# Emitting side work in step with the matrix products, and loading four groups of small vectors earlier

## The chip, the cores and the metric

The kernel runs on one core of one Trainium2 chip. The metric is device time in microseconds (us), the median of several runs of the whole kernel: 2437.35 us before the change, from 2432.09 to 2441.47 over three runs. The profile is of one further execution, which took 2433.36 us.

## The reference

The program is two networks, one after the other, on 256 tokens of width 1024 in float32. The first has two layers and a second stream of 256 context tokens; its even layer mixes with windowed attention beside a gated linear recurrence, its odd layer with retention. The second has two layers that mix gated delta-rule heads with windowed attention, each followed by a feed-forward part with a short convolution. What the change touches is this:

```python
# both networks: every sublayer is scaled, shifted and gated by vectors of a condition
m_lat = jnp.split((cond_lat @ mod_w[layer] + mod_b[layer])[:, None, :], 6, axis=-1)
h_lat = modulate(rms_norm(x, norm_g[layer, 0]), m_lat[0], m_lat[1])   # h * (1 + scale) + shift
x = x + m_lat[2] * y_lat
x = x + m_lat[5] * swiglu(modulate(...), ffn_w_in[layer], ffn_w_out[layer])
# even mixer: the query and key heads (64 wide) are normalised and multiplied by head weights
k_ctx = kv_heads(pc['a_k'], qk_g[1])
q_lat = apply_rope(attn_q_heads(p['a_q'], qk_g[0]), cos, sin)
```

The product of the condition with `mod_w` (called modulation here) has 1024 rows and 6144 columns per layer. The second network has the same with `w_ada`. It also has short vectors per layer: the norm weights of its attention's queries and keys (64 each), 16 sinks, and two vectors of 8 for the decay of its delta-rule heads.

## The kernel before

Every matrix product keeps float32 accuracy by three TensorE passes: each operand is split into a high and a low part, and hi·hi, hi·lo and lo·hi are added in PSUM (`mm3`, L190 to L192; the same three passes by hand in `fm_block`, L272 to L274). A weight tile of 128x1024 (512 KB) is fetched by a DMA that SyncE (SP) issues (`wload`, L177, tile `raw`, four buffers), ScalarE (ACT) casts its high part (`whi`, L181), and VectorE (DVE), or for some tiles GpSimd (POOL), subtracts to get the low part (`wlo`, L183).

The first modulation is a prologue on TensorE (`modulate_first`): four quarters `q`, each with `mbig` tiles of `mod_w`, followed by the tiles of the even layer's input weight for the same quarter of the contraction. A second set, for the even layer's later sublayers, runs by `mod_round` (L365). The modulation of the three layers that follow (called M1, M2, M3 in the code; three rounds of 2048 columns each) is spread over the even layer's feed-forward part, the odd layer and the odd layer's feed-forward part. It is a generator of 288 pieces (`mod_sums`): each fetches a 256 KB tile `mraw` (four buffers) and adds it, scaled by the condition, to an accumulator `macc` of 128x512, on DVE (L387, 280 of them) or, for the first of each eight, on ACT (L389). After 32 pieces a round ends: matmuls with a tile of ones (L393) add up the four accumulators of the round, a bias is added (`mraw`, L414), and the row is transposed into columns (L420, L423). There are four `macc` buffers, so the DVE additions of the next round wait for those matmuls.

`fill()` steps the generator. It is called once per weight tile, at the end of `wload`, and steps by `self.rate` pieces: 2.7 in the even layer's feed-forward part, 1.3 in the odd layer, 0.9 in the feed-forward part after it.

The order of instructions on each engine is not written by hand: the program emits them in a sequence, and a scheduler of the compiler places them per engine, with the emission as its priority. Each engine then runs its list in order. SP's list of DMA issues is such a list too, and the transfers of one queue are served in the order of issue.

The feed-forward part works in groups of hidden columns: gate and up products with the tokens as columns (`fm_block`), then a down-projection in two halves of 512 output columns (`proj_tm`), each into four PSUM banks, one per 128 tokens. DVE multiplies each bank by the gate (`res`, L494), which frees it.

In the even mixer `even_prep` (L850) loads the head weights `qkg` right before they are used: two DMAs that repeat 64 numbers over heads and partitions, 128x8x64 and 128x2x64. POOL multiplies by them (`qn`, L867). In the second network `bcast_rows` (L600) loads each short vector over 128 partitions where its layer begins: `sgq`, `sgk`, `ssink`, `alog` and `dtb`.

## Time and profile before

| | |
|---|---|
| median of three runs | 2437.35 us (2432.09 to 2441.47) |
| the profiled execution | 2433.36 us |
| its span, first to last instruction | 2431.5 us |
| TensorE matmuls busy | 2318.9 us (95%) |
| TensorE weight loads busy | 1954.7 us (80%) |
| VectorE busy | 1501.8 us (62%) |
| ScalarE busy | 1034.9 us (43%) |
| GpSimd busy | 751.5 us (31%) |
| mean granted TensorE clock | 0.978 of full speed |
| DMA | 399.77 MB, mean 164 GB/s |

TensorE is the engine that hardly rests: what it does not do in 2431.5 us is 112.6 us. So what an edit can save lies in these idle stretches, and in those where the granted clock is below 1. Busy time of the other engines counts only where TensorE waits for them. In the rows further on, a timeline row gives the start of an instruction (or of several alike, xN), how long they took, the engine, the line, and in brackets how long the engine was idle before it and what ended that.

### The profile page before, as it was taken

How to read it: one execution, taken by the hardware profiler on the slowest of the kernel's cores; microseconds unless marked ns; L12 is line 12 of the kernel's file. 1: busy time of each engine (PE TensorE's matmuls, PEld its weight loads, DVE VectorE, ACT ScalarE, POOL GpSimd, SP SyncE). 2: the span in 40 equal slices, each digit the busy share in tenths (PEclk: the TensorE clock that was granted, in tenths of full speed). 3: DMA queues.
4: the chain of work that ended last, by engine and by line, in shares of the span. 5: the costliest groups of instructions: out<-in, count | busy, mean ns of one | idle time of the engine just before them, and what ended most of it. 6: DMA issues, size and time to landing. Idle time of an engine off the chain costs nothing.

```text
span 2431.5 us, 38487 instructions
## 1 busy us (share of the span) xinstructions
PE 2318.9 (95%) x15032; PEld 1954.7 (80%) x15032; DVE 1501.8 (62%) x2398; ACT 1034.9 (43%) x1626; POOL 751.5 (31%) x554
## 2 busy tenths in 40 slices
PE   7889999998998999998999999998999999999999
PEld 6667778776786987877988987678997887778997
DVE  3677748767357747456434887356764888445763
ACT  3545425321223433334444654244444654344442
POOL 1544431112113123223443462133122462214112
PEclk9999999999999999999999999999999999999999
DMA  8333336777466737456655543254665552344664
GB/s 277 110 121 106 122 123 216 240 228 235 126 208 217 250 119 234 139 163 212 188 184 148 158 126 116 87 161 148 191 186 147 162 135 82 116 130 154 186 189 139
DMA packets 305898, 399.77 MB, mean 164 GB/s; under 512 B 38052, under 2 KB 203860, under 8 KB 303668
## 3 DMA queue, kind: packets, MB, share of 16 engines
q1 hardware_dynamic: 303540, 397.18, 52.5%
q8 instruction: 118, 1.93, 0.3%
q14 instruction: 64, 0.52, 0.1%
q10 hardware_dynamic: 2176, 0.13, 0.1%
HBM read 394.51 MB, written 2.74 MB: 163 GB/s over the span
## 4 chain that ended last, share of the span: by engine, by line
PE 74%; DVE 9%; DMA 8%; issue 4%; POOL 3%; ACT 1%; SPq 1%; POOLq 0%; DVEq 0%; ACTq 0%
PE acc L190 11%; PE acc L192 11%; PE acc L191 11%; PE acc L272 9%; PE acc L274 9%; PE acc L273 9%; DMA mraw<-in_w_ada_dram 5%; DVE macc L387 2%; DVE wlo L183 2%; DMA qkg<-in_attn_qk_norm_g_dram 1%; PE sm L1763 1%; PE rc L1751 1%; DVE pre L1609 1%; PE sm L1765 1%; PE rc L1753 1%
## 5 line engine op out<-in xcount | busy, mean ns | idle before, releaser
L181 ACT CAST whi<-raw 128x1024 fp32r<-128x1024 f32 (+1 forms) x528 | 550.7, 1046 | 615.1 <-PE acc L192 322.4
L183 DVE TENSOR_TENSOR wlo<-raw,whi 128x1024 fp32r<-128x1024 f32 x379 | 510.8, 1351 | 428.9 <-ACT whi L181 418.3
L183 POOL TENSOR_TENSOR wlo<-raw,whi 128x1024 fp32r<-128x1024 f32 (+1 forms) x149 | 369.3, 2478 | 1042.2 <-ACT whi L181 1023.8
L272 PE MATMUL acc<-hTh,whi 128*128 128x256 f32 (+1 forms) x1888 | 591.7, 313 | 12.6 <-DVE res L494 11.2
L274 PE MATMUL acc<-hTh,wlo 128*128 128x256 f32 (+1 forms) x1888 | 590.9, 313 | 2.8 <-DVE wlo L183 2.8
L273 PE MATMUL acc<-hTl,whi 128*128 128x256 f32 (+1 forms) x1888 | 589.4, 312 | 0.0
L272 PEld LDWEIGHTS acc<-hTh,whi 128*128 128x128 f32 x1888 | 357.9, 190 | 42.8 <-ACT whi L181 14.3
L274 PEld LDWEIGHTS acc<-hTh,wlo 128*128 128x128 f32 x1888 | 357.7, 190 | 29.8 <-DVE wlo L183 3.8
L273 PEld LDWEIGHTS acc<-hTl,whi 128*128 128x128 f32 x1888 | 358.1, 190 | 24.6 <-issue 3.2
L190 PE MATMUL acc<-whi,hTh 128*128 128x512 f32 (+2 forms) x992 | 334.4, 339 | 2.3 <-DVE rt L1126 0.7
L192 PE MATMUL acc<-whi,hTl 128*128 128x256 f32 (+2 forms) x992 | 331.1, 336 | 1.4 <-DVE hTl L168 0.9
L191 PE MATMUL acc<-wlo,hTh 128*128 128x512 f32 (+2 forms) x992 | 332.1, 336 | 0.0
L387 DVE SCALAR_TENSOR_TENSOR macc<-mraw,sil,macc 128x512 f32<-128x512 f32 x280 | 237.1, 857 | 78.6 <-DMA mraw<-in_w_ada_dram 45.2
L190 PEld LDWEIGHTS acc<-whi,hTh 128*128 128x128 f32 x992 | 187.9, 190 | 28.6 <-issue 6.1
L192 PEld LDWEIGHTS acc<-whi,hTl 128*128 128x128 f32 x992 | 187.0, 189 | 24.7 <-issue 2.0
L191 PEld LDWEIGHTS acc<-wlo,hTh 128*128 128x128 f32 x992 | 187.7, 189 | 21.7 <-issue 2.3
L191 PE MATMUL acc<-wlo,hidh 128*128 128x512 f32 x440 | 173.2, 395 | 0.0
L192 PE MATMUL acc<-whi,hidl 128*128 128x512 f32 x440 | 172.7, 395 | 0.0
L190 PE MATMUL acc<-whi,hidh 128*128 128x512 f32 x440 | 171.6, 396 | 1.0 <-ACT macc L389 0.8
L190 PEld LDWEIGHTS acc<-whi,hidh 128*128 128x128 f32 x440 | 82.5, 187 | 22.9 <-ACT macc L389 1.6
L192 PEld LDWEIGHTS acc<-whi,hidl 128*128 128x128 f32 x440 | 82.5, 187 | 20.1
L191 PEld LDWEIGHTS acc<-wlo,hidh 128*128 128x128 f32 x440 | 82.5, 187 | 19.9
(479 smaller groups left out, 3230.0 us busy)
## 6 DMA issues: line engine op xcount, KB each, us to landing
raw<-in_w_in_dram SPq DMA_DIRECT2D x112, 512.0 KB
mraw<-in_w_ada_dram SPq DMA_DIRECT2D x192, 256.0 KB
raw<-in_ffn_w_in_dram SPq DMA_DIRECT2D x88, 512.0 KB
raw<-in_w_up_dram SPq DMA_DIRECT2D x88, 512.0 KB
mraw<-in_mod_w_dram SPq DMA_DIRECT2D x96, 256.0 KB
raw<-in_odd_w_in_dram SPq DMA_DIRECT2D x48, 512.0 KB
raw<-in_ffn_w_out_dram SPq DMA_DIRECT2D x44, 512.0 KB
raw<-in_w_down_dram SPq DMA_DIRECT2D x44, 512.0 KB
```

The costliest lines, as they stand in the source:

```text
L181: nc.scalar.copy(hi, raw)
L183: eng.tensor_tensor(lo, raw, hi.bitcast(F32), ALU.subtract)
L190: mm(out, lhsT=ah, rhs=bh, start=start, stop=False)
L191: mm(out, lhsT=ah, rhs=bl, start=False, stop=False)
L192: mm(out, lhsT=al, rhs=bh, start=False, stop=stop)
L272: mm(out, lhsT=wh[:, s], rhs=hh[:, t0:t1], start=k == 0, stop=False)
L273: mm(out, lhsT=wh[:, s], rhs=hl[:, t0:t1], start=False, stop=False)
L274: mm(out, lhsT=wl[:, s], rhs=hh[:, t0:t1], start=False, stop=k == 7)
L387: nc.vector.scalar_tensor_tensor(accs[g, m], raw, v[:, k:k + 1], accs[g, m], ALU.mult, ALU.add)
L1609: nc.vector.scalar_tensor_tensor(pre[:, fb, s:], pa[:, fb, :256 - s], dcv[:, tap, blk:blk + 1], pre[:, fb, s:], ALU.mult, ALU.add)
L1751: mm(pv[r, s], lhsT=self.R[pr][r, u], rhs=self.kf[pr][r, u], start=True, stop=first)
L1753: mm(pv[r, s], lhsT=self.wT[pr][:, u, r], rhs=S[g][:, i], start=False, stop=True)
```

## The change

Three edits, which don't depend on each other:

1. `fill` is called in `mm3`, per product, with the product's columns, and no longer per weight tile. A piece is emitted for every 2048 / rate columns. `fm_block` calls `mm3`, so that its products count too; its three passes are the same, in another order. The rates become 1.3, 1.0 and 1.0.
2. `qkg` is loaded in `modulate_first`, at the third quarter (q = 2), and no longer in `even_prep`.
3. The ten short vectors of the second network's two layers are loaded in `setup2`, at the start of the odd layer's feed-forward part.

```diff
--- before.py
+++ after.py
@@ -181,7 +181,6 @@
         nc.scalar.copy(hi, raw)
         eng = nc.gpsimd if self.gran % self.pool_every == 0 else nc.vector
         eng.tensor_tensor(lo, raw, hi.bitcast(F32), ALU.subtract)
-        self.fill()
         return hi, lo
 
     def mm3(self, out, ah, al, bh, bl, start, stop):
@@ -190,6 +189,7 @@
         mm(out, lhsT=ah, rhs=bh, start=start, stop=False)
         mm(out, lhsT=ah, rhs=bl, start=False, stop=False)
         mm(out, lhsT=al, rhs=bh, start=False, stop=stop)
+        self.fill(int(np.prod(bh.shape[1:])))
 
     def proj_tm(self, h, tbs, w, c0, cw, evac, rows=None, kbs=None, tail=0):
 
@@ -265,13 +265,10 @@
     def fm_block(self, h, t0, t1, wt, fb, out):
 
         s = slice(fb * P, fb * P + P)
-        mm = self.nc.tensor.matmul
         for k in range(8):
             wh, wl = wt(k)
             hh, hl = h(k)
-            mm(out, lhsT=wh[:, s], rhs=hh[:, t0:t1], start=k == 0, stop=False)
-            mm(out, lhsT=wh[:, s], rhs=hl[:, t0:t1], start=False, stop=False)
-            mm(out, lhsT=wl[:, s], rhs=hh[:, t0:t1], start=False, stop=k == 7)
+            self.mm3(out, wh[:, s], wl[:, s], hh[:, t0:t1], hl[:, t0:t1], k == 0, k == 7)
 
     def fm_pair(self, h, T, w, c0):
 
@@ -396,11 +393,11 @@
                 self.mod_cols(M, r, pa, range(len(vs)), self.t(self.mod_pool, [P, 512], tag="mraw", bufs=4))
             yield
 
-    def fill(self):
-
-        self.credit += self.rate
-        while self.credit >= 1:
-            self.credit -= 1
+    def fill(self, cols):
+
+        self.credit += self.rate * cols
+        while self.credit >= 2048:
+            self.credit -= 2048
             next(self.todo, None)
 
     def mod_cols(self, M, r, pa, ms, row):
@@ -850,10 +847,7 @@
     def even_prep(self, ap, ke, raw, qT, kT):
 
         nc, I = self.nc, self.I
-        gain = self.t(ap, [P, 10, 64], tag="qkg")
-        g2 = I["attn_qk_norm_g"][0]
-        for i, n0, n1 in ((0, 0, 8), (1, 8, 10)):
-            nc.sync.dma_start(gain[:, n0:n1], g2[i].unsqueeze(0).unsqueeze(0).to_broadcast([P, n1 - n0, 64]))
+        gain = self.qkg
         for tb in (2, 3, 0, 1):
             lat = tb < 2
             r3 = raw[tb][:, :640].rearrange("p (h d) -> p h d", d=64)
@@ -985,6 +979,7 @@
         ps = ExitStack()
         pp = ps.enter_context(self.tc.tile_pool(name="pp", bufs=1, side="right", reuse_waits="tile"))
         self.scratch([], None)
+        self.qkg = self.t(pp, [P, 10, 64], tag="qkg")
         xT = self.t(self.npool, [P, 8, 512], tag="xT")
         for tb in TBS:
             for i, pt in enumerate(self.norm_fm_rows((src[tb],), self.npool)):
@@ -1023,6 +1018,9 @@
                             g = 64 * s + 32 * j
                             nc.tensor.matmul(pa[g:g + 32, :P], lhsT=cond[:, k0 + i], rhs=raw[:, i, s, j * P:j * P + P],
                                              start=k0 + i == 0, stop=k0 + i == 7)
+            if q == 2:
+                for i, n0, n1 in ((0, 0, 8), (1, 8, 10)):
+                    nc.sync.dma_start(self.qkg[:, n0:n1], I["attn_qk_norm_g"][0, i].unsqueeze(0).unsqueeze(0).to_broadcast([P, n1 - n0, 64]))
             row = self.t(self.npool, [P, P], tag="mrow", bufs=2)
             nc.vector.tensor_tensor(row, pa[:, :P], bias[:, q], ALU.add)
             pt = self.bank("mod")
@@ -1084,7 +1082,7 @@
         TBS = [0, 1, 2, 3]
         h = self.normed()
         self.todo = chain.from_iterable(self.mod_sums(m, r) for m, rs in ((M1, (0, 1, 2)), (M2, (0, 1, 2)), (M3, (0, 1, 2))) for r in rs)
-        self.rate = 2.7
+        self.rate = 1.3
         self.pool_every = 4
         self.ffn(h, TBS, I["ffn_w_in"][0], I["ffn_w_out"][0], x, lambda p: {tb: self.gate(p, M["dram"], tb // 2, 5, 2) for tb in (0, 2)},
                  (x, lambda: [self.modpair(M1["cols"], m, 0, 1, self.vcol("ng", 2)) for m in range(2)]))
@@ -1176,11 +1174,11 @@
         I = self.I
         h = self.normed()
         done()
-        self.rate = 1.3
+        self.rate = 1.0
         self.pool_every = 4
         self.odd(h, x, M)
         h = self.normed()
-        self.rate = 0.9
+        self.rate = 1.0
         self.pool_every = 2
         self.setup2(room("c2"))
         self.open_h(room("h2"), 256)
@@ -1194,6 +1192,9 @@
         self.rcos = self.t(cp, [P, 2, 16], tag="rcos")
         self.rsin = self.t(cp, [P, 2, 16], tag="rsin")
         self.convs = []
+        self.vec2 = [{nm: self.bcast_rows(cp, I[f"{src}_2"][l], w, f"{nm}{l}")
+                      for nm, src, w in (("sgq", "swa_q_norm", 64), ("sgk", "swa_k_norm", 64), ("ssink", "swa_sinks", 16),
+                                         ("alog", "dn_a_log", 8), ("dtb", "dn_dt_bias", 8))} for l in range(2)]
         self.identr = self.t(cp, [P, P], F32R, tag="identr")
         nc.vector.tensor_copy(self.identr, self.ident)
         self.swmask = self.t(cp, [P, 256], F32R, tag="swmask")
@@ -1351,9 +1352,7 @@
 
 
         nc, I = self.nc, self.I
-        gq = self.bcast_rows(ap, I["swa_q_norm_2"][l], 64, "sgq")
-        gk = self.bcast_rows(ap, I["swa_k_norm_2"][l], 64, "sgk")
-        sink = self.bcast_rows(ap, I["swa_sinks_2"][l], 16, "ssink")
+        gq, gk, sink = (self.vec2[l][nm] for nm in ("sgq", "sgk", "ssink"))
         nsink = self.t(ap, [P, 16], tag="snsink")
         nc.vector.tensor_scalar(nsink, sink, -1.0, None, ALU.mult)
         nc.vector.tensor_tensor(gk[:, 16:], gk[:, 16:], gq[:, 16:], ALU.mult)
@@ -1554,8 +1553,7 @@
     def gates(self):
 
         net, nc, I, l = self.net, self.nc, self.net.I, self.l
-        al = net.bcast_rows(self.op, I["dn_a_log_2"][l], 8, "alog")
-        db = net.bcast_rows(self.op, I["dn_dt_bias_2"][l], 8, "dtb")
+        al, db = (net.vec2[l][nm] for nm in ("alog", "dtb"))
         beta, g, a, e, gc, neg, k1 = (self.cols8[nm] for nm in ("beta", "g", "kss", "ke", "gc", "neg", "k1"))
         wide = lambda v: v.unsqueeze(1).to_broadcast([P, 2, 8])
         nc.scalar.activation(beta, self.abr[:, :, 8:], AF.Tanh, scale=0.5)
```

The lists of the engines move at these places. First SP's list around the head weights. Before, they come last of the even mixer's loads (`k_even` and `k_imask` are its constants), ahead of the first `mraw` of the second modulation:

```order
L150 DMA k_even_748<-in_k_even_dram 128x768
L150 DMA k_imask_750<-in_k_imask_dram 128x256
L856 DMA qkg_758<-in_attn_qk_norm_g_dram 128x8x64
L856 DMA qkg_758<-in_attn_qk_norm_g_dram 128x2x64
L364 DMA mraw_1122<-in_mod_w_dram 128x2048
```

After, they come in the prologue, behind the last `mbig` of q = 2 and ahead of that quarter's first input weight and of the `mbig` tiles of q = 3:

```order
L1014 DMA mbig_513<-in_mod_w_dram 128x2x256 x2
L1023 DMA qkg_117<-in_attn_qk_norm_g_dram 128x8x64
L1023 DMA qkg_117<-in_attn_qk_norm_g_dram 128x2x64
L177 DMA raw_544<-in_even_w_in_dram 128x2x512
L1014 DMA mbig_575<-in_mod_w_dram 128x2x256 x2
L1014 DMA mbig_586<-in_mod_w_dram 128x2x256 x2
```

The two transfers moved 16 places ahead. Next TensorE's list near the first group's down-projection in the even layer's feed-forward part. Before, the ones matmuls (`mod<-macc`) that end a round stand in the gate and up products (`hTh`, `hTl`), 53 matmuls ahead of the first matmul of the down-projection (`hidh`):

```order
L273 MATMUL acc_4906<-hTl_110,whi_4866 128x512
L274 MATMUL acc_4906<-hTh_109,wlo_4867 128x512
L393 MATMUL mod_4518<-macc_4870,ones_754 32x512
L393 MATMUL mod_4518<-macc_4768,ones_754 32x512
L393 MATMUL mod_4518<-macc_4614,ones_754 32x512
L393 MATMUL mod_4518<-macc_4519,ones_754 32x512
L272 MATMUL acc_4974<-hTh_109,whi_4934 128x512
L273 MATMUL acc_4974<-hTl_110,whi_4934 128x512
```

After, they stand behind 12 matmuls of the down-projection:

```order
L189 MATMUL acc_5009<-whi_5015,hidh_3815 128x512
L190 MATMUL acc_5009<-wlo_5016,hidh_3815 128x512
L191 MATMUL acc_5009<-whi_5015,hidl_3816 128x512
L390 MATMUL mod_4543<-macc_4921,ones_757 32x512
L390 MATMUL mod_4543<-macc_4796,ones_757 32x512
L390 MATMUL mod_4543<-macc_4664,ones_757 32x512
L390 MATMUL mod_4543<-macc_4544,ones_757 32x512
L189 MATMUL acc_5010<-whi_5015,hidh_3815 128x512
L190 MATMUL acc_5010<-wlo_5016,hidh_3815 128x512
```

So the four accumulators come free later. Third VectorE's list, at the evictions of that down-projection's first half (`res`). Before, the round's additions are through when the first `res` stands there, and 22 additions of the next round come between the fourth `res` and the evictions of the second half (the first six of them here):

```order
L494 TENSOR_TENSOR res_5269<-acc_5030,gate_3811 128x512
L494 TENSOR_TENSOR res_5272<-acc_5031,gate_3811 128x512
L494 TENSOR_TENSOR res_5275<-acc_5032,gate_3813 128x512
L414 TENSOR_TENSOR mraw_5491<-mod_5040,mraw_5491 128x512
L494 TENSOR_TENSOR res_5278<-acc_5033,gate_3813 128x512
L387 SCALAR_TENSOR_TENSOR macc_5503<-mraw_5552,sil_90,macc_5503 128x512
L387 SCALAR_TENSOR_TENSOR macc_5503<-mraw_5555,sil_90,macc_5503 128x512
L387 SCALAR_TENSOR_TENSOR macc_5503<-mraw_5564,sil_90,macc_5503 128x512
L387 SCALAR_TENSOR_TENSOR macc_5503<-mraw_5567,sil_90,macc_5503 128x512
L387 SCALAR_TENSOR_TENSOR macc_5503<-mraw_5570,sil_90,macc_5503 128x512
L387 SCALAR_TENSOR_TENSOR macc_5503<-mraw_5631,sil_90,macc_5503 128x512
```

After, 23 additions of the round stand ahead of the first `res`, a few among the four, and two behind them; then four `wlo` and the evictions of the second half follow:

```order
L384 SCALAR_TENSOR_TENSOR macc_5438<-mraw_5451,sil_90,macc_5438 128x512
L384 SCALAR_TENSOR_TENSOR macc_5438<-mraw_5472,sil_90,macc_5438 128x512
L491 TENSOR_TENSOR res_5256<-acc_5009,gate_3811 128x512
L491 TENSOR_TENSOR res_5259<-acc_5010,gate_3811 128x512
L384 SCALAR_TENSOR_TENSOR macc_5438<-mraw_5484,sil_90,macc_5438 128x512
L384 SCALAR_TENSOR_TENSOR macc_5438<-mraw_5496,sil_90,macc_5438 128x512
L491 TENSOR_TENSOR res_5262<-acc_5011,gate_3813 128x512
L384 SCALAR_TENSOR_TENSOR macc_5438<-mraw_5536,sil_90,macc_5438 128x512
L491 TENSOR_TENSOR res_5265<-acc_5012,gate_3813 128x512
L384 SCALAR_TENSOR_TENSOR macc_5438<-mraw_5548,sil_90,macc_5438 128x512
L384 SCALAR_TENSOR_TENSOR macc_5438<-mraw_5560,sil_90,macc_5438 128x512
```

The additions have moved from behind the four `res` to the stretch ahead of them.

## Rows read from the trace of the kernel before

**Rows 1.** page part 1, TensorE: busy us, share of span, instructions.
```profile
PE 2318.9 (95%) x15032; PEld 1954.7 (80%) x15032; DVE 1501.8 (62%) x2398; ACT 1034.9 (43%) x1626; POOL 751.5 (31%) x554
```

**Rows 2.** windows: busy us of PE, PEld, DVE, ACT, POOL; clock, DMA share, GB/s.
```profile
100.00:150.00 50.00, 38.61 (x262) 33.45 (x262) 44.37 (x46) 30.61 (x52) 37.25 (x24) 0.90 0.24 74
550.00:600.00 50.00, 39.31 (x172) 30.45 (x171) 33.42 (x41) 9.81 (x11) 12.12 (x8) 0.92 0.74 237
750.00:800.00 50.00, 39.99 (x205) 33.13 (x204) 39.70 (x59) 17.11 (x33) 16.20 (x17) 0.86 0.70 222
```

**Rows 3.** timeline of PE: start, us, operation [idle before <-what ended it].
```profile
90.28 1.94 PE L365 MATMUL mod<-mraw,cond 128*32 128x512 f32 x8 [6.47 <-DMA mraw<-in_mod_w_dram]
135.25 0.86 PE L787 MATMUL rc<-A,Bp 128*32 128x64 f32 x24 [10.97 <-DVE A L769]
599.16 0.76 PE L272 MATMUL acc<-hTh,whi 128*128 128x512 f32 x1 [9.77 <-DVE res L494]
777.87 1.94 PE L393 MATMUL mod<-macc,ones 128*32 128x512 f32 x8 [5.15 <-DVE macc L387]
1666.89 2.48 PE L466 MATMUL sm<-diag,x 128*128 128x128 f32 x10 [5.19 <-DVE sgk L1359]
```

**Rows 4.** timeline of SP, DVE and POOL around the head weights.
```profile
66.20 1.02 SPq L856 DMA_DIRECT2D qkg<-in_attn_qk_norm_g_dram  x2
77.48 0.82 DVE L866 TENSOR_TENSOR qn<-araw,rr 128x640 f32<-128x640 f32 x1
87.83 1.53 POOL L867 TENSOR_TENSOR qn<-qn,qkg 128x640 f32<-128x640 f32 x1 [10.99 <-DMA mraw<-in_mod_w_dram]
```

**Rows 5.** DMA packets in 69:78, 78:87 and 30:40 us.
```profile
DMA packets 888, 0.29 MB, mean 32 GB/s; under 512 B 816, under 2 KB 886, under 8 KB 887
DMA packets 1088, 1.36 MB, mean 151 GB/s; under 512 B 509, under 2 KB 997, under 8 KB 997
DMA packets 3381, 3.54 MB, mean 354 GB/s; under 512 B 198, under 2 KB 3124, under 8 KB 3380
```

**Rows 6.** timeline of SP, ACT and PE, 38 to 53 us.
```profile
38.98 0.37 SPq L177 DMA_DIRECT2D raw<-in_even_w_in_dram  x1
46.28 1.05 ACT L181 CAST whi<-raw 128x1024 fp32r<-128x1024 f32 x1 [4.61 <-DMA raw<-in_even_w_in_dram]
51.29 1.52 PE L1024 MATMUL mod<-mbig,cond 128*32 128x128 f32 x48 [0.37 <-PE mod L1029]
52.74 0.50 PE L190 MATMUL acc<-whi,hTh 128*128 128x512 f32 x1
```

**Rows 7.** timeline of PE and DVE around the down-projection of the first 512 columns.
```profile
506.65 1.06 PE L393 MATMUL mod<-macc,ones 128*32 128x512 f32 x8
519.39 0.39 PE L190 MATMUL acc<-whi,hidh 128*128 128x512 f32 x1
554.30 1.28 DVE L494 TENSOR_TENSOR res<-acc,gate 128x512 f32<-128x512 f32 x2
555.13 0.47 PE L190 MATMUL acc<-whi,hidh 128*128 128x512 f32 x1 [0.76 <-ACT macc L389]
598.33 1.28 DVE L494 TENSOR_TENSOR res<-acc,gate 128x512 f32<-128x512 f32 x2
```

**Rows 8.** timeline of DVE at the end of the even layer.
```profile
752.65 4.09 DVE L387 SCALAR_TENSOR_TENSOR macc<-mraw,sil,macc 128x512 f32<-128x512 f32 x4
772.66 0.68 DVE L494 TENSOR_TENSOR res<-acc,gate 128x512 f32<-128x512 f32 x1
790.88 0.69 DVE L168 TENSOR_TENSOR hTl<-hf,hTh 128x512 fp32r<-128x512 f32 x1 [0.40 <-ACT hTh L167]
```

**Rows 9.** timeline of SP and ACT early in the second FFN.
```profile
1119.58 0.34 SPq L1241 DMA_DIRECT2D cvr<-in_ffn_conv_b_dram  x1
1123.73 0.40 SPq L177 DMA_DIRECT2D raw<-in_ffn_w_in_dram  x1
1132.99 1.05 ACT L181 CAST whi<-raw 128x1024 fp32r<-128x1024 f32 x1 [0.48 <-PE acc L274]
```

## The prediction

> **What bounds the kernel now.** I read the busy times first: TensorE works 2318.9 of 2431.5 us [rows 1], so the whole change can move only its 112.6 us of idle time, and the stretches at a lower clock. Second, the busy times in stretches of 50 us: in 550 to 600 and in 750 to 800 TensorE is busy for 39 to 40 of 50 us at a granted clock of 0.92 and 0.86, and in 100 to 150 for 38.6 us at 0.90 while VectorE is busy for 44.4 us [rows 2]. Third, TensorE's timeline, for what ended each long idle stretch. Five of them touch the change [rows 3]: 6.47 us until 90.28 for an `mraw` of the prologue's second modulation; 10.97 us until 135.25 for VectorE; 9.77 us until 599.16 for a `res` eviction; 5.15 us until 777.87 for a modulation addition; and 5.19 us until 1666.89 at the start of the second network's second layer. That is 37.6 us, the most that the named places hold. Last the queues: who waits for the head weights, and how fast their packets go.
>
> **The change, part by part.** All terms are made against the profiled execution, 2433.36 us (its span is 2431.5); the median of the runs shown is 2437.35, so I take off the same sum from the median. A gain is written +.
>
> *Head weights.* Before, the two loads are issued at 66.20. VectorE has its factor of `qn` ready at 78.30 (77.48 + 0.82), and POOL multiplies at 87.83: 9.5 us of waiting [rows 4]. That wait goes, since the weights are there. What is late next is `qn` itself, which needs the first products. The load is 10 x 64 numbers over 128 partitions, so 1280 packets of 256 bytes, 0.33 MB. In 69 to 78 us, where hardly anything else is on the queue, 816 packets under 512 B go in 9 us, 91 per us, at 32 GB/s together; in 30 to 40 us the stream of weights runs at 354 GB/s [rows 5]. The new place is in that stream, behind the last `mbig` of q = 2 and in front of the weight tile now issued at 38.98 and cast at 46.28, and of q = 3's `mbig`, whose matmuls start at 51.29 [rows 6]. At 91 per us the 1280 packets hold up what is behind them for 14 us; by their bytes at 354 GB/s for 0.9 us. The tile of q = 2 has 5 us to spare (its cast ends at 47.3, the products start at 52.74), q = 3's modulation has none. So TensorE's first products end between 0.9 and 14 us later. In the one case `qn` starts 9.5 us earlier and both stretches behind it (6.47 and part of 10.97) shrink: at most +9. In the other the products feed `qn` 14 us later than its 78.30, so 4.5 us later than now; with the mean of both packet paces below, -8. Nearest is the row that shows these very packets, which puts the delay at 9 (behind 5 us of slack) to 14 us, about as much as the wait that goes. I take 0, from -8 to +9.
>
> The Trainium skill ("DMA: Bandwidth & Descriptors", "Why small descriptors are slow (HBM only)") puts a 256-byte descriptor at 11 cycles where its data need 8; that would make this load an estimated 1.3 us of the stream (0.33 MB x 11/8 at 354 GB/s), and the term about +8. The 32 GB/s of [rows 5] speak against it by a factor of ten, so I don't go by it; as a rival it stands below.
>
> *Emission by products: the down-projection of the first hidden group.* The rate hardly changes: 2.7 pieces per weight tile before, and 1.3 x 4096 / 2048 = 2.6 after. What changes is where the additions stand. Before, the ones matmuls end at 507.71 (506.65 + 1.06), 28 additions follow on VectorE, and the first `res` comes right behind them at 554.30: 46.6 us, 1.66 for each addition with what stands between. Then 22 more additions stand in front of the next `res`, which comes at 598.33, and TensorE waits for it 9.77 us [rows 3, 7]. After the change only two stand there, so this wait goes; the evictions come right at the end of their products. What is late next is the first `res`. The ones matmuls now stand 12 matmuls behind the start of the down-projection; by its start at 519.39 and a matmul each 0.233 us (519.39 to 555.13 less 2 us for ones and waits, for 144 of them) that is 522.2, and 523.3 at their end. The 23 additions in front of the first `res` take 38.2 us at 1.66 each, so it comes at 561.5, 7.2 us later than now; at 1.33 us (fifteen additions stand in the 20 us from 752.65 to 772.66 [rows 8]) it comes at 554, on time. The bank of that `res` is needed at once, by the next half's products (they start at 555.13, after a wait of 0.76). So I count a new wait of 4 us, the middle between none and 8 (7.2 + 0.76), in place of 0.76. The gain is 9.77 + 0.76 - 4 = 6.5, of which I keep +6, since three additions among the four `res` hold up the others; from -1 (the wait at its longest, and 4 us more behind it) to +11.
>
> *The end of the even layer.* A burst of 15 additions between evictions becomes one of 14, and the ones matmuls that wait 5.15 us at 777.87 no longer stand there. But VectorE is the engine that this place waits for: from the first of the last four `res` at 772.66 to the first split of the next layer's input at 790.88 it has 18.2 us [rows 8], nearly without a gap. In that stretch stand six additions and one bias addition before, and eight additions after; the other work is the same. TensorE's wait moves from one instruction to another. I take 0; from -4 (those eight waiting for their transfers at 1.33 us, in place of 0.75) to +5 (the wait that goes).
>
> *The odd layer and the feed-forward part after it.* Rounds are shifted there too, by up to 28 additions, but from the layer's last projections on, VectorE's additions stand as before. With no row to tell, 0, from -4 to +3, the size of a wait such as that at 777.87, less what is beside it. Even attention is reordered because the head weights come earlier: 0, within 5 us either way, half of the wait at 135.25.
>
> *Short vectors.* They take about 1 us from the waits at the layer starts (most of the 5.19 us at 1666.89 is for a norm on POOL that stays). They add ten issues of 0.4 us; SP is idle from 1119.92 to 1123.73, which covers nearly all of them. But ten transfers of 128 packets are 1280 packets again: 14 us at the pace above, from 1120.5 to 1134.5, ahead of the weight tile issued at 1123.73, which is cast at 1132.99 [rows 9]. The tile then lands 2 to 4 us late, of which the split tiles ahead of TensorE take a part. -1; from -6 to +2.
>
> **Sum.** 0 + 6 + 0 + 0 + 0 - 1 = +5: 2428 us for an execution like the profiled one, and 2432 against the median of 2437.35. The bad ends together, added as squares, are 14 us, the good ones 13. With 1 to 2 us for the spread of a median of runs that reach from 2432 to 2441, the forecast's own range is 2418 to 2448.
>
> **Rivals.**
> - *The head weights cost only their bytes inside the stream.* For it: the pace of 91 packets per us is from a stretch where few transfers were outstanding. Against it: 1280 packets needed until 87.83, 21.6 us from their issue. Then this term is +9, the first `res` at the faster pace of additions gives +10, the vectors 0: -19, so 2418.
> - *Small packets block the queue; slower.* In 78 to 87 us, where other transfers share the engines, 509 packets under 512 B go, 57 per us [rows 5]. At that pace 1280 take 22 us. In the prologue q = 3's `mbig` come 22 us late, less the 9.5 us of the old wait, -12; in the second feed-forward part the tile of 1132.99 comes about 11 us late. With +6 from the down-projection that is -17: 2454. It decides from the point where the pace inside a loaded queue is below 91 per us. Against it: packets that share a queue's engines with others may well have been the tail of a transfer that was already nearly through.
> - *The additions stay where they hurt.* The rate is the same, the scheduler follows the emission, and a new wait of 7 us at the first `res`, with the additions among the four, takes back what the old one gave; with 0 for the rest that is 2437, no change.
>
> **How the numbers follow.** Forecast 0.47, first rival 0.25, second 0.15, third 0.13. A difference of 0.5% (12 us) is what a measurement of this kernel can tell from none. Below 2425: the first rival and a quarter of the forecast, 0.37. Above 2449.5: the second rival and a small part of the forecast, 0.16. The rest, 0.47, within. Range 2416 to 2449, which leaves out the far side of the second rival and a little of the first.
>
> **What would show it.** In the profile after: the head weights' wait at POOL gone, and TensorE's first product of q = 2 at 53 to 55 (first rival), at 58 to 64 (forecast) or later (second); its idle time until the down-projection's second half, now 0.76, at 1 to 7 us, and the 9.77 us gone; the stretch 770 to 795 with TensorE as idle as now; the cast now at 1132.99 late by 2 to 4 us. The forecast is wrong if the first products are not late, or if the second half of the down-projection waits for more than 10 us.

## The result and the profile after

| | before | after |
|---|---|---|
| median, first chip (four runs each) | 2436.76 us (2432.09 to 2441.47) | 2455.59 us (2451.29 to 2457.4) |
| median, second chip (20 and 4 runs) | 2430.35 us (2427.16 to 2435.12) | 2443.45 us (2437.34 to 2445.31) |
| span of the profiled execution, first chip | 2431.5 us | 2452.0 us |

The changed kernel is slower: by a factor of 1.0075 (95% interval 1.005 to 1.0099) on the first chip and 1.0052 (1.0036 to 1.0069) on the second. Forecast was 2432, with a range to 2449.

The busy times of the engines, which answer to [rows 1]:

```profile
PE 2328.0 (95%) x15032; PEld 1962.9 (80%) x15032; DVE 1512.3 (62%) x2398; ACT 1037.0 (42%) x1628; POOL 753.8 (31%) x554
```

TensorE and VectorE have as many instructions as before. Of the 20.5 us that the span has grown, 9.1 are busy time (the same matmuls at a lower clock, 0.974 in the mean in place of 0.978) and 11.4 idle time. Where, the windows tell; the columns are those of [rows 2]. After:

```profile
100.00:150.00 50.00, 39.03 (x238) 33.26 (x237) 43.70 (x44) 27.71 (x48) 36.71 (x23) 0.86 0.31 103
550.00:600.00 50.00, 44.63 (x184) 35.45 (x183) 25.95 (x27) 9.32 (x10) 11.59 (x7) 0.93 0.63 199
750.00:800.00 50.00, 39.92 (x186) 31.39 (x186) 35.43 (x50) 16.48 (x32) 21.25 (x17) 0.92 0.65 204
950.00:1000.00 50.00, 45.65 (x216) 36.27 (x215) 40.88 (x47) 13.33 (x18) 15.04 (x10) 0.97 0.77 247
1000.00:1050.00 50.00, 44.38 (x223) 37.30 (x222) 27.67 (x39) 18.13 (x28) 12.25 (x11) 0.93 0.52 158
```

and before, for the two windows that [rows 2] don't have:

```profile
950.00:1000.00 50.00, 47.84 (x216) 38.74 (x216) 36.66 (x45) 16.57 (x23) 12.24 (x10) 1.00 0.67 211
1000.00:1050.00 50.00, 50.00 (x256) 42.07 (x255) 19.83 (x29) 17.64 (x27) 12.17 (x11) 1.00 0.33 99
```

550 to 600 us has improved (TensorE busy for 44.6 in place of 39.3 us), as forecast. 950 to 1050 us, the odd layer, has become worse by 7.8 us of idle time, and its clock has fallen from 1.00 to 0.97 and 0.93. The table below follows the loss through the kernel. It takes the starts of the 3624 matmuls that read a low part of a weight (`wlo`), of which each trace has all, and subtracts the start of the same one in the trace of before, which is from the first chip. A kernel that is equal to before up to some place is there still up to 6 us off (the short vectors alone, up to 1116 us; the wide load, everywhere), so a step from one column to the next says more than a level. The kernels are those of the experiments; `q` is the quarter of the prologue at which the head weights are loaded.

| matmul | 41 | 121 | 401 | 641 | 721 | 881 | 1041 | 1081 | 1201 | 1241 | 1441 | 1841 | 3624 |
|---|---|---|---|---|---|---|---|---|---|---|---|---|---|
| start before, us | 58 | 139 | 380 | 542 | 613 | 726 | 838 | 870 | 963 | 995 | 1138 | 1324 | 2425 |
| changed kernel | +13.6 | +4.9 | +10.4 | +10.4 | +5.4 | +11.5 | +7.3 | +7.3 | +9.3 | +22.5 | +23.3 | +19.6 | +20.4 |
| the same, second chip | +12.0 | +3.3 | +5.7 | +5.3 | -0.6 | +2.7 | -2.1 | -2.1 | -0.2 | +12.4 | +13.5 | +9.9 | +3.8 |
| head weights alone | +11.7 | +3.0 | +7.6 | +7.5 | +4.9 | +4.9 | +3.7 | +3.7 | +1.6 | +1.9 | +2.0 | +2.3 | -1.0 |
| emission alone | -0.4 | -1.9 | -2.6 | -3.1 | -7.2 | -2.8 | -6.3 | +0.3 | +0.4 | +0.2 | +0.2 | +1.1 | -1.2 |
| short vectors alone | -0.7 | -1.9 | -1.4 | -1.1 | -0.9 | -0.9 | -1.9 | -1.9 | -3.8 | -3.3 | -2.4 | -5.1 | -10.1 |
| head weights at q = 0 | +17.6 | +6.5 | +10.8 | +10.9 | +7.5 | +11.7 | +8.0 | +14.5 | +15.3 | +15.2 | +16.5 | +13.1 | +7.2 |
| all, 128 packets | -1.3 | -10.0 | -6.1 | -6.4 | -13.0 | -8.9 | -13.8 | -13.8 | -13.5 | -1.9 | -1.5 | -5.4 | -10.3 |
| 128 packets, early | +0.2 | -8.6 | -4.2 | -4.3 | -7.1 | -7.1 | -7.9 | -7.9 | -7.4 | -7.6 | -8.4 | -7.9 | -11.8 |
| 128 packets, old place | -0.5 | -8.8 | -9.9 | -10.0 | -11.8 | -11.8 | -12.6 | -12.6 | -13.0 | -13.3 | -12.8 | -12.0 | -11.3 |

The changed kernel loses 13 us in the prologue, has won back 9 by 139 us, loses 6 more in the even mixer, wins 5 at the first down-projection, loses 6 before 726 us, wins 4 by 838 us, loses 2 by 963 us and 13 more by 995 us, and wins 4 where the second network begins.

The prologue, with timeline rows that answer to [rows 4, 6]; behind them the DMA row of 36 to 44 us, and the window of the same stretch, before and after (columns of [rows 2]):

```profile
32.14 2.17 SPq L1023 DMA_DIRECT2D qkg<-in_attn_qk_norm_g_dram  x2
62.55 2.79 PE L1019 MATMUL mod<-mbig,cond 128*32 128x128 f32 x48 [5.83 <-issue]
65.26 0.80 PE L189 MATMUL acc<-whi,hTh 128*128 128x512 f32 x1
75.97 0.50 PE L189 MATMUL acc<-whi,hTh 128*128 128x512 f32 x1 [0.17 <-ACT hTh L1037]
91.95 2.48 POOL L861 TENSOR_TENSOR qn<-qn,qkg 128x640 f32<-128x640 f32 x1 [1.54 <-DVE qn L860]
```

```profile
DMA packets 678, 0.21 MB, mean 27 GB/s; under 512 B 645, under 2 KB 677, under 8 KB 677
```

```profile
36.00:44.00 8.00, 7.63 (x90) 6.46 (x91) 3.18 (x9) 3.02 (x5) 2.25 (x1) 1.00 1.06 359
36.00:44.00 8.00, 7.63 (x96) 6.33 (x97) 3.20 (x9) 2.08 (x4) 0.00 (x0) 1.00 0.10 27
```

The head weights are issued at 32.14. In 36 to 44 us the queue then moves 645 small packets, and 27 GB/s in all, where it moved 359 before; the busy share of the DMA engines (a sum over packets, which can pass 1) falls from 1.06 to 0.10. So, as the trace counts it, it is not the time of the packets on these engines that holds up the weights; what does is not shown. The modulation of q = 3 starts at 62.55 in place of 51.29, the first product of q = 2 at 65.26 in place of 52.74 [rows 6], and that of q = 3 at 75.97 in place of 62.61. POOL multiplies at 91.95, 4.1 us later than before, without a wait for the weights.

The down-projection, for [rows 7]:

```profile
531.06 1.06 PE L390 MATMUL mod<-macc,ones 128*32 128x512 f32 x8
568.08 1.28 DVE L491 TENSOR_TENSOR res<-acc,gate 128x512 f32<-128x512 f32 x2
568.91 0.76 PE L189 MATMUL acc<-whi,hidh 128*128 128x512 f32 x1 [5.37 <-DVE res L491]
602.82 1.39 DVE L491 TENSOR_TENSOR res<-acc,gate 128x512 f32<-128x512 f32 x2 [1.26 <-PE acc L191]
```

The first `res` comes 37 us behind the ones matmuls and keeps the next half waiting for 5.37 us; the evictions at 602.82 come with no wait of TensorE for them. At the layer's end TensorE now waits for other things than in [rows 3], and for an `act` before:

```profile
724.73 0.80 PE L189 MATMUL acc<-whi,hidh 128*128 128x512 f32 x1 [3.27 <-DVE act L542]
796.36 1.86 PE L463 MATMUL sm<-diag,x 128*128 128x128 f32 x7 [7.84 <-ACT hf L477]
```

The odd layer has two new waits, of PE for DVE (`rt`, a rotated query; `ovl`, the low part of v). The DVE rows between them show what stands ahead of `ovl`:

```profile
983.33 0.77 PE L189 MATMUL acc<-whi,hTh 128*128 128x512 f32 x1 [3.30 <-DVE rt L1124]
1002.56 0.75 DVE L384 SCALAR_TENSOR_TENSOR macc<-mraw,sil,macc 128x512 f32<-128x512 f32 x1 [5.15 <-DMA mraw<-in_w_ada_dram]
1004.36 3.61 DVE L384 SCALAR_TENSOR_TENSOR macc<-mraw,sil,macc 128x512 f32<-128x512 f32 x2
1007.89 0.68 DVE L168 TENSOR_TENSOR ovl<-acc,ovh 128x512 fp32r<-128x512 f32 x1
1008.63 0.79 PE L189 MATMUL acc<-whi,hTh 128*128 128x512 f32 x1 [5.62 <-DVE ovl L168]
```

An addition at 1002.56 has waited 5.15 us for its `mraw`, two more take 3.61 us, and `ovl` stands behind them. So VectorE's own wait for a tile that nothing needs yet is most of TensorE's 5.62 us. TensorE's first matmul after it takes 0.79 us, double the 0.39 us of one in [rows 7].

### The profile page after: what moved, and what is told of

The parts are those of the page before. It is cut to its first block, busy times and chain, and to the rows that moved or that the text cites. A ratio compares the mean times of both kernels' runs of the same rounds, so it can differ in the third digit from the quotient of the medians.

```text
span 2452.0 us, 38471 instructions
## 1 busy us (share of the span) xinstructions
PE 2328.0 (95%) x15032; PEld 1962.9 (80%) x15032; DVE 1512.3 (62%) x2398; ACT 1037.0 (42%) x1628; POOL 753.8 (31%) x554
## 4 chain that ended last, share of the span: by engine, by line
PE 74%; DMA 9%; DVE 9%; issue 3%; POOL 2%; ACT 1%; SPq 1%; POOLq 0%; DVEq 0%; ACTq 0%
PE acc L189 20%; PE acc L191 20%; PE acc L190 20%; DMA mraw<-in_w_ada_dram 5%; DVE macc L384 2%; DVE wlo L183 2%; PE sm L463 1%; DMA mraw<-in_mod_w_dram 1%; PE sm L1761 1%; PE rc L1749 1%; DMA mbig<-in_mod_w_dram 1%; DMA raw<-in_even_w_in_dram 1%; DVE pre L1607 1%; PE sm L1763 1%; PE rc L1751 1%
## 5 line engine op out<-in xcount | busy, mean ns | idle before, releaser
L189 PE MATMUL acc<-whi,hTh 128*128 128x512 f32 (+2 forms) x992 | 337.9, 342 | 10.1 <-DVE ovl L168 5.6
L384 DVE SCALAR_TENSOR_TENSOR macc<-mraw,sil,macc 128x512 f32<-128x512 f32 x280 | 246.3, 888 | 89.7 <-DMA mraw<-in_w_ada_dram 50.0
L191 PEld LDWEIGHTS acc<-whi,hidl 128*128 128x128 f32 x440 | 83.5, 190 | 20.5
```

The lines of the kernel that those rows point to most:

```text
L189: mm(out, lhsT=ah, rhs=bh, start=start, stop=False)
L191: mm(out, lhsT=al, rhs=bh, start=False, stop=stop)
L384: nc.vector.scalar_tensor_tensor(accs[g, m], raw, v[:, k:k + 1], accs[g, m], ALU.mult, ALU.add)
```

## The experiments

The first eight ran on the second chip, the last four (those with 128 packets) on a third, each against runs of before on its own chip, whose median was 2430.1 to 2430.5 us; a difference in us is the ratio less one, times 2430. The first four expectations give their times on the first chip's scale, from 2437 us.

**The three parts, each alone.** The kernel before with one part of the diff above; head weights first.

> The kernel before with the head weights moved into the prologue, nothing else. Theory A (the 1280 small packets hold up the weight stream): the first products of q = 2 and q = 3 come 10 to 13 us late, some of it is won back at the old waits at 90 and 135 us, and 7 to 10 us are left at the start of the even layer's feed-forward part (near 380 us) and at the end: 2444 to 2447 us. Rival B (the early load is harmless, the lag at 380 us in the changed kernel comes with the other edits): within 3 us of before.

Measured: 1.0031 (1.0021 to 1.0041), +7.5 us. Two PE rows and the first multiply on POOL:

```profile
62.02 2.79 PE L1022 MATMUL mod<-mbig,cond 128*32 128x128 f32 x48 [3.87 <-issue]
74.12 0.51 PE L190 MATMUL acc<-whi,hTh 128*128 128x512 f32 x1 [0.15 <-ACT hTh L1040]
90.14 2.48 POOL L864 TENSOR_TENSOR qn<-qn,qkg 128x640 f32<-128x640 f32 x1 [1.55 <-DVE qn L863]
```

q = 3's modulation is 11 us late (62.02 for 51.29), its products 11.5 (74.12; 62.61 before), `qn` 2.3 us. The lag is 3.0 us at 139 us and 7.6 at 380: the second half of it arises in the even mixer, where the order of the matmuls is another one. Theory A holds, at the lower end of its price.

> The kernel before with the emission by products at rates 1.3, 1.0 and 1.0, nothing else. Theory A: no lag until 500 us, 5 us won at the first group's down-projection, some 12 us lost in the odd layer's projections between 960 and 1010 us, where the pieces come faster than before: +6 to +10, 2443 to 2447 us. Rival B (the edit is neutral, as predicted, and the odd layer's loss comes from the shift in time by the prologue): within 5 us of before, no idle stretch of 5 us for the splits of v.

Measured: 1.0012 (1.0003 to 1.0021), +2.9 us. By this number rival B holds (within 5 us, no wait of 5 us for the splits of v), but the edit is not neutral. The down-projection wins 4.2 us, there is no loss at 960 to 1010 us, but one of 6.6 us between 838 and 870, where `okl` and `okh`, splits of k, are late; PE's rows and the window:

```profile
844.26 0.39 PE L189 MATMUL sm<-oqh,okh 128*128 128x256 f32 x1 [2.05 <-ACT okh L167]
846.43 0.58 PE L191 MATMUL sm<-oqh,okl 128*128 128x256 f32 x1 [1.41 <-DVE okl L168]
840.00:860.00 20.00, 16.54 (x93) 14.78 (x92) 16.69 (x23) 7.25 (x12) 5.00 (x6) 0.83 0.81 275
```

The two waits make 3.5 us; the clock there is 0.83, and the slower matmuls behind the waits bring the loss to 6.6.

> The kernel before with the second network's ten short vectors fetched ahead, nothing else. Theory A (their old place cost more than their new one): 2 to 4 us won at the start of the second network, 2433 to 2436 us, and TensorE not late at 1140 us. Rival B (small packets block the queue here as in the prologue): 2 to 6 us lost between 1120 and 1150 us, 2438 to 2443 us.

Measured: 0.998 (0.9971 to 0.999), -4.9 us. Theory A: TensorE is 0.9 us later at 1138 against 995, and gains 2.7 until 1324. An ACT row after the ten loads, and PE's wait at the second network's second layer; behind them the DMA row of 1119 to 1125 us in the kernel before, and VectorE's rows where the second network begins, also before:

```profile
1131.82 1.05 ACT L181 CAST whi<-raw 128x1024 fp32r<-128x1024 f32 x1 [0.44 <-DMA raw<-in_ffn_w_in_dram]
1660.67 2.69 PE L466 MATMUL sm<-diag,x 128*128 128x128 f32 x11 [5.19 <-DVE diag L460]
```

```profile
DMA packets 150, 0.10 MB, mean 17 GB/s; under 512 B 33, under 2 KB 136, under 8 KB 149
1313.49 0.21 DVE L1359 TENSOR_TENSOR sgk<-sgk,sgq 128x48 f32<-128x48 f32 x1 [1.61 <-DMA sgk<-in_swa_k_norm_dram]
1313.62 0.68 DVE L168 TENSOR_TENSOR hTl<-hf,hTh 128x512 fp32r<-128x512 f32 x1
```

A weight tile is 0.44 us late for its cast, no more: the queue moved only 17 GB/s there before, so the small packets had little to hold up. The wait of 5.19 us at the second layer's start is as long as in [rows 3]; it was never for the vectors. At the first layer's start it is otherwise. Before, VectorE stood 1.61 us for `sgk` in front of the split `hTl` that TensorE needs; and TensorE's granted clock was 0.61 in 1313 to 1317 us. With the vectors ahead that wait is gone, and the clock at the same place (1309 to 1313 us) is 1.00. The six kernels here that load them ahead win 2.3 to 4.0 us between 1138 and 1324 us, and the six others lose 0.2 to 0.9.

**The odd layer at its old rate.** The emission alone with one rate changed:

```diff
-        self.rate = 1.0      # odd layer
+        self.rate = 0.65     # 1.3 pieces per weight tile of 4096 columns, as before
```

> The emission by products alone, with the odd layer at 0.65 in place of 1.0, which is the old 1.3 pieces per weight tile of 4096 columns. Theory A (the loss in the odd layer is the rate, 2.0 pieces per tile): the 12 us between 960 and 1010 us go, the 5 us won at the first down-projection stay: 2430 to 2435 us. Rival C (the loss is the finer emission, at any rate): the same loss as with 1.0, 2443 to 2447 us.

Measured: 1.0011 (1.0001 to 1.0021), +2.7 us. Theory A falls: the loss at 838 to 870 us is there (7.1 us), and another of 5.6 us between 963 and 995, which 1.0 does not have. The faster rate is not the cause.

The parts add to +5.5 us, and the whole is more. The order tells why. How many of the 15032 matmuls of the trace stand ahead of the ones matmuls of each of the ten rounds:

```text
before              2797 2935 3202 3406 3802 4126 4306 5074 5774 6060
emission alone      2804 2959 3262 3550 3880 4174 4424 5074 5774 6060
changed kernel      2804 2959 3262 3550 3880 4174 4936 5156 5774 6060
with q = 0          2804 2959 3262 3550 3880 4174 4424 5074 5774 6060
```

With the emission by products and the head weights early at q = 2, the seventh falls from the end of the even layer to 512 matmuls later; with the head weights alone all ten stand as before. (The expectations below count rows of the compiler's list, which has fewer rows than the trace has matmuls: 3849 there is 4936 here, and 3351 is 4424.) The additions of the next two rounds follow it. With the emission alone they run from 799 to 857 us and from 924 to 975; in the changed kernel from 903 to 951 and from 957 to 1014, 18 of them between the outputs `opt` and the first eviction. Nothing in the odd layer's own code differs from the emission alone.

> The changed kernel once more, for a comparison on the same chip with the three kernels beside it, and with the parts measured alone (+7.6, +3 and -5 us, a sum of +5.6). Theory A (the parts don't add: with the early head weights the ones matmuls of the seventh round stand 490 matmuls later on TensorE, and the additions behind them meet the odd layer's splits of v): +15 to +20 us, the lag jumps by 10 us or more near 1000 us. Rival B (the first comparison was 10 us off): +4 to +8 us.

Measured: 1.0052 (1.0036 to 1.0069), +12.6 us; the step between 963 and 995 us is 12.6 us. Theory A by that step; the total is a little below what it said. It is 7.1 us more than the parts, and that is nearly what the place of the loss makes: the emission alone loses 6.6 us at 838 to 870 us and nothing at 963 to 995, the changed kernel nothing at the first and 12.6 us at the second.

**Early head weights with the old place of the ones matmuls.**

```diff
-            if q == 2:
+            if q == 0:
```

> The changed kernel with the head weights loaded at the first quarter (q = 0) in place of the third. The scheduler then puts the ones matmuls of the seventh and eighth round back to where they stand with the emission alone (TensorE rows 3351 and 3981 in place of 3849 and 4056); nothing else of the odd layer's order is meant to change. Theory A (the odd layer's loss of 13 us hangs on that place): the jump near 1000 us is gone, about 7 us are lost near 850 us as with the emission alone, and with the small packets as dear in the prologue as before the total is +4 to +9 us. Rival C (the loss hangs on the late start, so that any lag of 10 us brings it): the jump near 1000 us stays, +15 to +20 us.

Measured: 1.0035 (1.0022 to 1.0048), +8.5 us. PE's rows at the splits of k, and the window before 1000 us:

```profile
857.82 0.39 PE L189 MATMUL sm<-oqh,okh 128*128 128x256 f32 x1 [1.69 <-ACT okh L167]
859.55 0.58 PE L191 MATMUL sm<-oqh,okl 128*128 128x256 f32 x1 [0.99 <-DVE okl L168]
980.00:1000.00 20.00, 19.37 (x84) 15.30 (x83) 13.71 (x15) 4.24 (x5) 4.14 (x4) 1.00 0.63 207
```

The step at 963 to 995 us is gone (-0.1), and the 6.5 us at 838 to 870 are back, though the kernel starts later than the changed one. So the place of the loss goes with the order, not with the lag.

**The emission and the short vectors, without the early head weights.**

> Emission by products and the ten short vectors ahead, the head weights at their old place. Theory A (no early head weights, so neither the prologue's loss nor the odd layer's): +3 - 5, so -4 to 0 us. Rival B (the edits of the odd layer's loss are the emission's own): +5 us or more.

Measured: 0.9982 (0.9973 to 0.9992), -4.4 us, as theory A says and no better than the short vectors alone. The short vectors and the emission together leave the seventh ones matmuls at 4424, so they do not move them by themselves.

**As many bytes in large packets at the early place.**

```diff
+            if q == 2:
+                for n0, n1 in ((0, 512), (512, 640)):
+                    nc.sync.dma_start(self.wide[:, n0:n1], I["even_w_in"][0, 0:P, n0:n1])
```

> The kernel before, with an added load at the place where the changed kernel loads the head weights: two transfers of the same 0.33 MB in rows of 2048 and 512 bytes from a weight matrix, 256 packets in place of 1280; they are not used, and the head weights stay at their old place. Theory A (the prologue's loss is the small packets that all read the same few addresses): the first products come at most 2 us late, within 2 us of before at 380 us and at the end. Rival B (any transfer at that place delays the stream, or the scheduler's new order does it): the products at 58 us come some 10 us late, 5 to 8 us left at 380 us.

Measured: 0.9996 (0.9986 to 1.0005). DMA packets in 36 to 44 us:

```profile
DMA packets 2384, 2.92 MB, mean 365 GB/s; under 512 B 145, under 2 KB 1841, under 8 KB 2384
```

Theory A: the same 0.33 MB at the same place leave the stream at 365 GB/s and cost nothing that can be measured. The order of the even mixer is nearly the one of before here, so this run says nothing on what another order costs.

**The head weights in 128 packets.** The 2 x 64 numbers are loaded once per partition, and repeated over the heads by two copies on POOL. Early:

```diff
+            if q == 2:
+                nc.sync.dma_start(self.qk2, I["attn_qk_norm_g"][0].unsqueeze(0).to_broadcast([P, 2, 64]))
+                nc.gpsimd.tensor_copy(self.qkg[:, 0:8], self.qk2[:, 0:1].to_broadcast([P, 8, 64]))
+                nc.gpsimd.tensor_copy(self.qkg[:, 8:10], self.qk2[:, 1:2].to_broadcast([P, 2, 64]))
```

> The kernel before with the head weights at the changed kernel's early place, but loaded as 128 packets of 512 bytes (the 2 x 64 numbers once per partition) and repeated over the heads by two POOL copies. Theory A (the price is the number of small packets): the first products are at most 2 us late, POOL multiplies some 8 us earlier than before (near 80 us), and the wait of 6.5 us for the prologue's mraw shrinks: -9 to -3 us. Rival B (the early place itself, or the scheduler's order that comes with it, costs): +4 us or more, as with the 1280 packets.

Measured: 0.9982 (0.9973 to 0.9992), -4.4 us. Against +7.5 with 1280 packets: the 11.9 us between the two are the packets. 8.6 us are won by 139 us, but 4.4 given back by 380, where the even mixer's order is another one, so rival B is right in part: the order that comes with the early place has a price of its own. Every kernel that loads the head weights early loses 2.4 to 5.5 us there, with either number of packets; of those that load them at the old place none loses more than 1.0.

At the old place, by the same copies in `even_prep`:

> The kernel before with the head weights at their old place, loaded as 128 packets of 512 bytes and repeated by two POOL copies. Theory A (what the old place cost was the 1280 packets, not the place): POOL's wait until 87.83 and TensorE's wait until 90.28 shrink by 6 to 9 us, and -8 to -3 us in all. Rival C (the wait is hidden anyway, since VectorE bounds the stretch to 150 us): 0 to -2 us.

Measured: 0.9973 (0.9963 to 0.9983), -6.6 us. POOL's first multiply:

```profile
77.94 2.48 POOL L868 TENSOR_TENSOR qn<-qn,qkg 128x640 f32<-128x640 f32 x1 [1.46 <-DVE qn L867]
```

It comes at 77.94 in place of 87.83 [rows 4], and nothing is given back (-8.8 at 139 us, -9.9 at 380). The wait was the packets, not the place.

> The changed kernel whole, with the head weights at its early place as 128 packets. The order of the later engines' lists is as in the changed kernel (the ones matmuls of the seventh round 490 matmuls late). Theory A (the odd layer's loss hangs on that order and not on the late start): no lag at 380 us, and still a jump of 10 us or more near 1000 us: +0 to +6 us in all. Rival C (the jump comes from starting 10 us late): no jump, -10 us or less in all.

Measured: 0.9988 (0.9979 to 0.9998), -2.9 us. This is the changed kernel, with its ones matmuls at the same rows, 10.0 us ahead at 139 us in place of 4.9 behind. PE's rows and the window of the odd layer:

```profile
959.62 0.48 PE L189 MATMUL acc<-whi,hTh 128*128 128x512 f32 x1 [2.67 <-DVE rt L1126]
984.70 0.80 PE L189 MATMUL acc<-whi,hTh 128*128 128x512 f32 x1 [6.79 <-DVE ovl L168]
980.00:1000.00 20.00, 15.30 (x60) 12.26 (x61) 15.19 (x20) 6.94 (x9) 3.37 (x2) 0.83 0.71 228
```

It waits 2.67 us for `rt` and 6.79 us for `ovl` and loses 11.6 us between 963 and 995 us, about as much as the changed kernel. The start has nothing to do with that step. The total came out below what theory A said, since it allowed nothing for the 9 us that the early load wins once it is cheap.

**The version that the experiments point to.** The short vectors ahead, the head weights at their old place in 128 packets, the emission as before.

> The kernel before with two things: the ten short vectors ahead, and the head weights at their old place as 128 packets. Theory A (both gains are real and lie in different places, so they add): -13 to -8 us, the fastest so far. Rival C (only the short vectors matter): -5 us, as alone.

Measured: 2417.17 us against 2430.14, 0.9946 (0.9931 to 0.9961), -13.1 us: both gains add, and it beats both kernels.

## Why the prediction was wrong

*Head weights: mechanism right, price wrong.* The text saw that 1280 packets of 256 bytes would hold up the weights for up to 14 us, that `qn` would be 4.5 us later than before in that case (it is 4.1), and bounded the term at -8. It then took 0. Alone the edit costs 7.5 us, in two steps of the table: 3.0 us of lag at 139 us, and 4.5 more by 380. The first step that failed is the "I take 0": the 9.5 us of the old wait were set against the delay, though in the case that the nearest row showed, `qn` is the later for it. The second is "Even attention is reordered because the head weights come earlier: 0": 4.4 us go there also with 128 packets, where nothing is late and the order alone is another one. It lay within the 5 us that the text allowed, but not at 0. The pace in the loaded queue is 81 packets per us (645 in 8 us), near the 91 of [rows 5], so the second rival's pace of 57 did not occur; the delay of q = 3 was 11.3 us. The sign on record for the prologue had pointed at that rival, with a first product of q = 2 at 65.26, later than the 58 to 64 of the forecast. The sum by the Trainium skill's rule fails by more: the Trainium skill ("DMA: Bandwidth & Descriptors", "Why small descriptors are slow (HBM only)") has 11 cycles for 8, and the measured pace is 27 GB/s of 354. The wide load shows that bytes are not it. Reading one address many times is not enough either: the 128 packets of 512 bytes all read the same 512 bytes, and the queue moved 341 GB/s with them in 34 to 38 us (361 before). Whether it is the packet's size, their number or both was not separated.

*The first down-projection: right.* The old wait of 9.77 us is gone, the new one is 5.37 (forecast 4, none to 8), and the gain is 5.0 us by the table, 4.2 with the emission alone (forecast 6).

*The end of the even layer: no gain, as said.* But 6 us are lost before 726 us, with a wait of 3.27 us for an `act`, which no term had; the emission alone has 4.4 of them. Of the changed kernel's 6 us 4 are won again by 838 us.

*The odd layer: the step that failed most.* "With no row to tell, 0, from -4 to +3": it lost 13 us. The text had seen that rounds shift there "by up to 28 additions"; what then stands behind them was not priced. In the changed kernel the last additions still stand among the splits of v and the outputs, up to 1014 us, where before they end at 975. The price could have been bounded from rows: an addition in such a burst takes 1.33 to 1.66 us, so four or five of them ahead of a split that TensorE needs at once make a wait of 5 to 7 us, and the end of the even layer had shown a lower clock around such a wait (0.86 in 750 to 800 [rows 2]). Measured are two waits, 3.30 and 5.62 us; what is left of the 13 us is mostly slower matmuls. What moved the additions to where they cost most is the early load of the head weights together with the new emission: it changed where the scheduler put the ones matmuls of one round. The emission alone pays 6.6 us for its burst, at 838 to 870. Why the scheduler places that round so late is not settled, nor whether the short vectors have a part in it, since no run has the other two edits without them; that its place decides is shown by the load at q = 0, and that the late start does not by the whole change with 128 packets.

*The short vectors: sign wrong.* -1 was forecast, +4.9 measured. The ten loads are nearly free where they are now (0.44 us for a tile), so the delay of 2 to 4 us did not come: the term took the pace of the prologue, but the queue had hardly anything to hold up there (17 GB/s before). And "about 1 us from the waits at the layer starts" was too little: 2.7 us are won by 1324 us, where VectorE no longer waits for `sgk`. The rest lies later, in steps of 1 to 3 us of the size by which traces of one kernel differ, and is not settled.

*The rivals.* The second, with the packets, had the right side and nearly the right time (2454), but that is luck: of its two losses the prologue's came, smaller (7.5 us alone, not 12), the second feed-forward part's 11 us did not, and the odd layer's 13 us, which it did not have, filled the gap. The third expected a gain that is taken back in the same place; it was taken back in the odd layer. Neither of the two signs on record that the forecast is wrong appeared: the first products were late, and the second half of the down-projection waited for 5.37 us, not for more than 10. The loss lay mostly where no sign had been set.

## What to carry to other kernels

When an edit lets a scheduler move work on an in-order engine, price each place where a burst has moved in front of something that TensorE waits for, also far from the edit; "no row to tell" is a place that has not been priced. Before a small transfer is fetched earlier, count its packets, and ask what is behind it in the queue: here the load in 128 packets won 6.6 us at the old place and 4.4 at the early one, and in 1280 packets it lost 7.5 by being early. Parts that were measured alone (+7.5, +2.9, -4.9) need not add up, where they share a schedule.

## What the runs showed of the hardware

- 0.33 MB in 1280 packets of 256 bytes, read from the same few addresses, took the weight queue from 359 to 27 GB/s in 36 to 44 us, with the DMA engines busy for a share of 0.10 in place of 1.06; with 256 packets of 2048 and 512 bytes from a matrix the queue stayed at 365 GB/s, and with 128 packets of 512 bytes at 341 in 34 to 38 us.
- Behind TensorE's waits of 3.27, 3.30, 5.37, 5.62 and 6.79 us the first matmul took 0.76 to 0.80 us in place of 0.39. With the emission alone, behind two waits of 3.5 us together, the granted clock was at the lower of its two levels (0.50) in 845 to 850 us, and the loss was 6.6 us; in the odd layer, two waits of 9.5 us together cost 11.6 with the whole change in 128 packets.
- Ten loads of 128 small packets each, 1018 of the packets in 1119 to 1125 us, delayed a weight tile by 0.44 us, in a place where the queue had moved 17 GB/s before; the 1280 small packets in front of the weight stream delayed the next modulation by 11 us.
